# The last tile's final norm: channels-by-tokens with a broadcast factor, or tokens-by-channels with one factor per partition

## The chip, the cores and the metric

The kernel runs on one core of one Trainium2 chip. The metric is the device time of one execution in microseconds (us); lower is better. Before the change it is 2097.62 us, the median of three runs (2097.12 to 2098.48).

## The reference, cut to what matters

One inference step of a one-layer decoder: 2048 prompt tokens (behind 16 learned meta tokens) and 8 sample tokens, each a vector of 1024 channels in float32. A layer norms the input, projects it, runs sliding-window attention beside a depthwise convolution, adds the result back, and goes through a two-matrix feed-forward block (1024 to 4096 to 1024). What the change touches is the last line for both groups of tokens:

```
def rmsnorm(x, g):
    xf = x.astype(jnp.float32)
    y = xf * lax.rsqrt(jnp.mean(xf * xf, axis=-1, keepdims=True) + EPS)
    return (y * g.astype(jnp.float32)).astype(x.dtype)

    x = x + hid @ w_down                                # end of the layer
    y_prompt = rmsnorm(xp, norm_f_g)[:, N_META:]
    y_sample = rmsnorm(xs, norm_f_g)
```

Each token has one factor, the reciprocal root of the mean of its 1024 squares; each channel has one gain `g`.

## The kernel before, in words

Activations lie transposed: channels on the 128 partitions (8 chunks of 128 for 1024 channels), tokens along the row. The 2056 tokens that go out are cut into five tiles of 384, 448, 448, 448 and 328 tokens (the last one holds 320 prompt tokens and the 8 sample tokens). Weights come as 128x1024 slabs, 424 of them, through SP's queue; each is split into a high and a low float32r part (`whi` by ScalarE, `wlo` by VectorE), and `pe_step` runs 24 matmuls with one slab into one PSUM bank.

The tiles go through the feed-forward block one after the other. Work that isn't TensorE's main stream (attention, convolution, norms) is written as generators that are advanced between the matmuls; a scheduler then sets each engine's order by priority and readiness. For the last tile nothing is left to run beside it at the end: after the last `down_step` the program runs the final norm alone.

`down_step` (g = 3) adds the last partial result to the residual `y = s["x2"][d]` on VectorE (L115, `t<-mm,t`), once for each of the 8 chunks, and counts `s["ydone"]`. `final_gen` of the last tile follows: `norm_stats` squares each chunk on ScalarE (L134, `m<-t`) and sums the squares on VectorE (L115, `ss`). `rstd` in its quick form then takes three blocks of at most 128 tokens: matmuls of `ss` with a column of ones put the sum of each token on a partition of its own (`st<-ones,ss`), ScalarE takes the root (`rq<-st,epst`), VectorE the reciprocal (L130), ScalarE scales an identity with it (`m<-idn,rq`), matmuls with ones spread the factors over all partitions (`st<-m,ones`), and ScalarE copies them to `rs` (L138). At last VectorE multiplies each chunk by gain and factor (L119, `t<-t,sm,rs`, 8 times 128x328), and each chunk is stored as 128 rows of 328 tokens, from SP's and ScalarE's queue in turn (L934, `y_out<-t`). The host puts the chunks back in order after the run.

A PSUM pool of 8 banks is shared: `mm` (3 banks, the main stream), `pt` and `s` (2 each, attention), `st` (1, small results). `bias` (128x2048) and `p` are buffers of the attention.

Of the kernel before, what the change touches and what calls it, by code (L numbers as in the profile page):

```python
# [7 lines left out]
F32 = mybir.dt.float32  # L8
F32R = mybir.dt.float32r
AF = mybir.ActivationFunctionType  # L10
ALU = mybir.AluOpType
PSUM = bass.MemoryType.PSUM

D = 1024
SEQ = 2048
NMETA = 16
NSMP = 8
# [9 lines left out]
NT = len(PT)  # L27
RT = [PT[i] + (NSMP if i == NT - 1 else 0) for i in range(NT)]
# [3 lines left out]
YO = [8 * sum(RT[:i]) for i in range(NT)]  # L32
TM = max(TI)
# [8 lines left out]
G1, G2, GF, CWT, CB, LG, LB, SK, SKR = 0, 8, 16, 24, 148, 152, 156, 160, 168  # L42
# [3 lines left out]
STEP = "step"  # L46
# [30 lines left out]
            self.step(DRAIN)  # L77


def trunk(tc, x_in, w_all, smalls, rel, ck, cv, sconv, y_out, kv_out, ck_out, cv_out, up_out, us_out):  # L80
    nc = tc.nc
    with ExitStack() as ctx:
        cp = ctx.enter_context(tc.tile_pool(name="cp", bufs=1))
        tp = ctx.enter_context(tc.tile_pool(name="tp", bufs=NSLOT))
        tm = ctx.enter_context(tc.tile_pool(name="tm", bufs=NTMP))
        sl = ctx.enter_context(tc.tile_pool(name="sl", bufs=3))
        at = ctx.enter_context(tc.tile_pool(name="at", bufs=1))
        dr = ctx.enter_context(tc.tile_pool(name="dr", bufs=1, space=bass.MemoryType.DRAM))
        pm = ctx.enter_context(tc.tile_pool(name="pm", bufs=3, space=PSUM))
        pa = ctx.enter_context(tc.tile_pool(name="pa", bufs=2, space=PSUM))  # L90
        p1 = ctx.enter_context(tc.tile_pool(name="p1", bufs=1, space=PSUM))

        def ahead(gen, off, cond=None):
            while True:
                try:
                    if off and (cond is None or cond()):
                        with tc.high_priority(off):
                            r = next(gen)
                    else:
                        r = next(gen)  # L100
                except StopIteration:
                    return
                yield r
# [13 lines left out]
        def stt(out, a, s, b, op0, op1):  # L117
            dcost(out, 0.06)
            return nc.vector.scalar_tensor_tensor(out, a, s, b, op0=op0, op1=op1)  # L119
# [23 lines left out]
        def slot(dt=F32, i=None):  # L143
            t = tp.tile([128, TS], dt, tag="t", name="t")
            return t[:, SHIFT[i]:] if i in SHIFT else t
# [15 lines left out]
        sm = tm.tile([128, NSMALL], F32, tag="sm", name="sm", bufs=1)  # L161
# [3 lines left out]
        idn = cp.tile([128, 128], F32, name="idn")  # L165
        make_identity(nc, idn)
        ones = cp.tile([128, 128], F32, name="ones")
        nc.vector.memset(ones, 1.0)
        epst = cp.tile([128, 1], F32, name="epst")
# [3 lines left out]
        bias = cp.tile([128, NH, 256], F32, name="bias")  # L173
# [37 lines left out]
        bg = Background(clock)  # L211
# [105 lines left out]
        def run_stats(gen, box):  # L317
            for r in gen:
                if r is None or r is STEP:
                    yield r  # L320
                else:
                    box.append(r)

        def norm_split(chunks, n, gcol, hi, lo, ready=None, quick=False, i=None):
            box = []
            yield from run_stats(norm_stats(chunks, n, ready, quick), box)
            rs = box[0]
            prev = None
            def fin(p):
                c, h = p  # L330
                tt(lo[c][:, :n], h[:, :n], f(hi[c][:, :n]), ALU.subtract)

            for c in range(8):
                h = tmp()
                stt(h[:, :n], chunks[c][:, :n], sm[:, gcol + c:gcol + c + 1], rs[:, :n], ALU.mult, ALU.mult)
                hi.append(slot(F32R, i))
                lo.append(slot(F32R, i))
                cpy(hi[c][:, :n], h[:, :n])
                yield
                if prev is not None:  # L340
                    fin(prev)
                    yield
                prev = (c, h)
            fin(prev)

        st = [dict() for _ in range(NT)]
# [12 lines left out]
        def norm1_gen(i):  # L359
            x = st[i]["x"] = load_x(i)  # L360
            yield STEP
            st[i]["h1h"], st[i]["h1l"] = [], []
            yield from norm_split(x, TI[i], G1, st[i]["h1h"], st[i]["h1l"], quick="a%d" % i in QUICK, i=i)

        def norm1_first():
# [22 lines left out]
            s["rs"] = slot()  # L388
            for _ in ahead(run_stats(norm_stats(x, n, quick="a0" in QUICK, gate=s["h1h"][7], out=s["rs"]), box), 2000):
                pass  # L390
# [330 lines left out]
        def conv_gen(i):  # L721
# [66 lines left out]
            yield STEP  # L788
            if "m%d" % i in QUICK:
                ps = misc(i < LNM)  # L790
# [20 lines left out]
            box = []  # L811
            yield from run_stats(rstd(ssum, r, 1.0 / 512, "l%d" % i in QUICK, i < LNM), box)
            rs = box[0]
# [66 lines left out]
        def norm2_gen(i):  # L880
            s = st[i]
            s["h2h"], s["h2l"] = [], []
            while "x2" not in s:
                yield STEP
            yield from norm_split(s["x2"], RT[i], G2, s["h2h"], s["h2l"], ready=lambda c: len(s["x2"]) > c,
                                  quick="b%d" % i in QUICK, i=i)

# [20 lines left out]
        def down_step(i, g, d, budget):  # L908
# [10 lines left out]
                flush()  # L919
            pe_step([t[:, :n] for t in s["hh"]], [t[:, :n] for t in s["hl"]], n, ev, budget, late=d == 0)  # L920

        def final_gen(i):
            s = st[i]
            n = RT[i]
            s.setdefault("ydone", 0)
            box = []
            yield from run_stats(norm_stats(s["x2"], n, ready=lambda c: s["ydone"] > c,
                                             quick="f%d" % i in QUICK), box)
            rs = box[0]
            for c in range(8):  # L930
                y = s["x2"][c]
                stt(y[:, :n], y[:, :n], sm[:, GF + c:GF + c + 1], rs[:, :n], ALU.mult, ALU.mult)
                q = (nc.sync, nc.scalar)[c % 2] if i == NT - 1 else nc.gpsimd
                q.dma_start(y_out[:, YO[i] + c * n:YO[i] + (c + 1) * n], y[:, :n])  # L934
                yield

        def bias_setup():
# [78 lines left out]
        for op in prog:  # L1016
# [6 lines left out]
            elif op[0] == "ff":  # L1023
                _, i, t, g, k = op
# [3 lines left out]
        gens = {}  # L1028
        nin = 0
        cat_alloc(0)  # L1030
        for op in prog:
            k = op[0]
            if k == "in":
                _, i, m = op
                if i == 0:
                    if nin == N1AT:
                        gens["n1"] = [bg.add(g1)]
                    if nin == BAT:
                        bias_setup()
                    nin += 1  # L1040
                win_step(i, m, 24 * (TI[i] / 2400.0) - 1.2 - 0.6, spare=i == 0 and nin in (4, 5))
            elif k == "in2":
                m = op[1]
                win_step(0, m, 24 * (TI[0] / 2400.0) - 1.2 - 0.6, keep=True)
                win_step(1, m, 24 * (TI[1] / 2400.0) - 0.6)
            elif k == "conv0":
                flush()
                gens["conv"] = [bg.add(ahead(conv_gen(0), HP0, lambda: "ln" in st[0])), bg.add(conv_pe_gen(0), True)]
            elif k == "attn0":
                flush()  # L1050
                gens["attn"] = [bg.add(attn_gen(0, range(j, PT[0] // BQ[0], NS0)), A0F) for j in reversed(range(NS0))]
            elif k == "out":
                _, i, m = op
                wout_step(i, m, ff_budget(i, False))
            elif k == "ff":
                _, i, t, g, c = op
                b = ff_budget(i, t == "u")
                if t == "u":
                    up_step(i, g * 8 + c, b)
                else:  # L1060
                    down_step(i, g, c, b)
            elif k == "bg":
                i = op[1]
                flush()
                cat_alloc(i)
                gens["attn"] = [bg.add(attn_gen(i, range(j, PT[i] // BQ[i], NS1))) for j in range(NS1)]
                if i == NT - 1:
                    gens["attn"].append(bg.add(sample_gen(i)))
                gens["conv"] = [bg.add(ahead(conv_gen(i), HPC, lambda: "ln" in st[i]))]
            elif k == "sync_bg":  # L1070
                flush()
                bg.drain(gens["attn"] + gens["conv"])
            elif k == "n1":
                gens["n1"] = [bg.add(norm1_gen(op[1]))]
            elif k == "sync_n1":
                bg.drain(gens["n1"])
            elif k == "n2":
                gens["n2"] = [bg.add(ahead(norm2_gen(op[1]), HPN if op[1] else HPN0))]
            elif k == "sync_n2":
                flush()  # L1080
                bg.drain(gens["n2"])
            elif k == "fin":
                gens["fin"] = [bg.add(ahead(final_gen(op[1]), HPF if op[1] == NT - 1 else 0))]
                if op[1] == NT - 1:
                    flush()
                    bg.drain()
# [14 lines left out]
HPC = 0  # L1101
HPN = 0
HPN0 = 300
HPF = 0
COV = 5
BAT = 1
WARM = 12
N1AT = 3
A0F = True
QUICK = ["a0", "a1", "l0", "m0", "b0", "f4"]  # L1110
NS0 = 2
NS1 = 1
NPB = 2
# [6 lines left out]
def _pack(inp):  # L1120
# [62 lines left out]


_OUTS = [
    ("y_out", (128, 8 * sum(RT))), ("kv_out", (128, 2, 128 + NSMP)), ("ck_out", (128, 1024)),
    ("cv_out", (128, 1024)), ("up_out", (128, 4, CW - 1)), ("us_out", (128, 4, NSMP, CW)),
]

# [38 lines left out]
```

## Time and profile before

| | us |
|---|---|
| median of three runs | 2097.62 |
| the profiled execution, its own time | 2097.54 |
| its span, first to last instruction | 2095.7 |
| TensorE matmul busy | 2068.3 (99%) |
| weight loads busy | 1961.5 (94%) |
| VectorE busy | 1525.2 (73%) |
| ScalarE busy | 1181.0 (56%) |
| DMA queue of SP, share of 16 engines' span | 32.5% |

The span runs from the first to the last instruction; the execution's own time is 1.84 us longer. Busy times can overlap between engines. TensorE's granted clock is full in nearly all of the span (mean 0.993). The end of the span, where TensorE has no more of its main stream, is a few microseconds long and is too short to be seen in these shares.

### The profile page before, as it was taken

What the parts mean: (1) busy time and instruction counts of PE and PEld (TensorE: products, weight loads), DVE (VectorE), ACT (ScalarE), POOL (GpSimd) and SP (SyncE); (2) the same over time, 40 slices, a digit from 0 to 9 for tenths busy, and PEclk for the clock granted to TensorE, in tenths of its full rate; (3) what the DMA queues carried; (4) which work ended last, traced back from release to release, by engine and by line L of the source; (5) the groups of instructions that cost most, each with busy time, mean ns of one, the idle gap of its engine ahead of it and who ended that gap; (6) DMA issues with size and microseconds to landing.
All of it is one profiled execution on the core that took longest, in us unless ns stands there. A gap on an engine that the chain in (4) does not pass through costs nothing.

```text
span 2095.7 us, 30054 instructions
## 1 busy us (share of the span) xinstructions
PE 2068.3 (99%) x11354; PEld 1961.5 (94%) x11354; DVE 1525.2 (73%) x2603; ACT 1181.0 (56%) x2154; POOL 55.8 (3%) x111
## 2 busy tenths in 40 slices
PE   9899999999999999999999999999999999999998
PEld 8688899999999999999999999999999999999997
DVE  7896798977858987658669886567797754564444
ACT  7577565667456456564454647555646465454443
POOL 3000000000000000000000000000011000000000
PEclk9899999999999999999999999999999999999999
DMA  7113233334532222234323222244433322444443
GB/s 209 47 37 111 100 122 104 128 114 160 179 111 101 101 101 101 101 136 162 129 104 108 101 101 101 101 172 150 142 117 112 123 105 101 151 162 151 151 143 105
DMA packets 77536, 254.39 MB, mean 121 GB/s; under 512 B 9661, under 2 KB 20037, under 8 KB 77392
## 3 DMA queue, kind: packets, MB, share of 16 engines
q1 hardware_dynamic: 72000, 238.08, 32.5%
q0 software_dynamic: 4672, 13.65, 2.3%
q8 instruction: 89, 1.46, 0.3%
q10 hardware_dynamic: 720, 0.76, 0.1%
q14 instruction: 55, 0.45, 0.1%
HBM read 241.97 MB, written 10.47 MB: 120 GB/s over the span
## 4 chain that ended last, share of the span: by engine, by line
PE 95%; DVE 2%; DMA 1%; ACT 1%; issue 0%; POOL 0%; SPq 0%; DVEq 0%; ACTq 0%; POOLq 0%
PE mm L159 89%; PE st L159 2%; PE pt L595 1%; PE s L159 1%; DVE t L119 1%; DMA bias<-skw 0%; DMA skw<-t 0%; DVE t L115 0%; PE cps L159 0%; DVE m L119 0%; ACT p L135 0%; DMA raw<-w_all 0%; DVE p L576 0%; DMA sm<-smalls 0%; ACT L134 0%
## 5 line engine op out<-in xcount | busy, mean ns | idle before, releaser
L159 PE MATMUL mm<-t,whi 128*128 128x448 f32 (+3 forms) x6560 | 1330.9, 349 | 3.1 <-ACT t L138 0.8
L159 PEld LDWEIGHTS mm<-t,whi 128*128 128x128 f32 x6560 | 1164.1, 188 | 58.2 <-DVE t L115 2.9
L138 ACT CAST whi<-raw 128x1024 fp32r<-128x1024 f32 x424 | 443.5, 1049 | 546.6 <-PE mm L159 430.2
L159 PE MATMUL mm<-t,wlo 128*128 128x448 f32 (+3 forms) x3280 | 702.6, 347 | 0.0
L115 DVE TENSOR_TENSOR wlo<-raw,whi 128x1024 fp32r<-128x1024 f32 x424 | 516.6, 1218 | 224.7 <-PE mm L159 123.5
L159 PEld LDWEIGHTS mm<-t,wlo 128*128 128x128 f32 x3280 | 587.9, 188 | 24.9
L119 DVE SCALAR_TENSOR_TENSOR t<-u,sm,t 128x448 f32<-128x448 f32 (+1 forms) x480 | 300.5, 645 | 3.5
L115 DVE TENSOR_TENSOR t<-mm,t 128x448 f32<-128x448 f32 (+2 forms) x200 | 116.5, 583 | 184.5 <-PE mm L159 181.4
L115 DVE TENSOR_TENSOR t<-m,t 128x448 fp32r<-128x448 f32 (+3 forms) x236 | 134.1, 581 | 25.8 <-ACT t L138 25.1
L138 ACT CAST t<-m 128x448 fp32r<-128x448 f32 (+3 forms) x236 | 125.3, 536 | 18.8 <-DVE m L119 14.6
L134 ACT ACTIVATE m<-mm 128x448 f32<-128x448 f32 (+2 forms) x176 | 90.2, 512 | 51.0 <-PE mm L159 49.5
L134 ACT ACTIVATE m<-t 128x448 f32<-128x448 f32 (+3 forms) x140 | 71.7, 542 | 61.7 <-DVE t L115 43.0
L134 ACT ACTIVATE m<-m 128x448 f32<-128x448 f32 (+3 forms) x164 | 90.1, 549 | 4.5 <-DVE m L115 0.6
L135 ACT ACTIVATE p<-p,nm 112x240 f32<-112x240 f32 (+3 forms) x152 | 72.3, 477 | 27.3 <-DVE nm L124 25.9
L576 DVE CUSTOM_DVE_ANT_0 p<-s,bias,sm 112x240 f32<-112x240 f32 (+3 forms) x152 | 61.1, 449 | 6.2 <-DMA bias<-skw 3.8
L134 ACT ACTIVATE p<-p,rd 112x240 f32<-112x240 f32 (+3 forms) x152 | 61.9, 476 | 3.9 <-DVE rd L130 3.5
L115 DVE TENSOR_TENSOR ss<-ss,m 128x448 f32<-128x448 f32 (+3 forms) x100 | 58.4, 584 | 6.3 <-ACT m L134 2.8
L934 POOL DMA_DIRECT2D y_out<-t x32 | 17.3, 543 | 1602.6 <-DVE t L119 1601.4
L130 DVE RECIPROCAL rs<-m 128x448 f32<-128x448 f32 (+2 forms) x15 | 41.6, 2776 | 23.9 <-ACT m L134 23.9
L119 DVE SCALAR_TENSOR_TENSOR t<-t,sm 128x384 f32<-128x384 f32 (+1 forms) x98 | 58.3, 612 | 0.9
L159 PE MATMUL mm<-cal,whi 128*128 128x448 f32 (+2 forms) x160 | 55.3, 347 | 0.2 <-DVE cal L115 0.2
L159 PE MATMUL mm<-cah,whi 128*128 128x448 f32 (+2 forms) x160 | 55.3, 347 | 0.0
(178 smaller groups left out, 1159.6 us busy)
## 6 DMA issues: line engine op xcount, KB each, us to landing
raw<-w_all SPq DMA_DIRECT2D x424, 512.0 KB, 3.2
t<-x_in SPq DMA_DIRECT2D x40, 224.0 KB, 4.6
y_out<-t POOLq DMA_DIRECT2D x24, 224.0 KB, 3.3
t<-x_in SPq DMA_DIRECT2D x16, 164.0 KB, 3.5
t<-x_in POOLq DMA_DIRECT2D x8, 224.0 KB, 4.3
t<-x_in SPq DMA_DIRECT2D x8, 200.0 KB, 4.6
t<-x_in SPq DMA_DIRECT2D x8, 192.0 KB, 3.8
y_out<-t POOLq DMA_DIRECT2D x8, 192.0 KB, 4.7
```

What stands on the lines that cost most here:

```text
L115: return nc.vector.tensor_tensor(out, a, b, op=op)
L119: return nc.vector.scalar_tensor_tensor(out, a, s, b, op0=op0, op1=op1)
L130: return nc.vector.reciprocal(out, a)
L134: return nc.scalar.activation(out, a, f, bias=bias, scale=scale)
L135: return nc.scalar.activation(out, a, f, bias=bias, scale=scale, accum_out=accum_out)
L138: return nc.scalar.copy(out, a)
L159: return nc.tensor.matmul(out, lhsT, rhs, start=start, stop=stop)
L576: nc.vector.tensor_tensor_reduce(out=p[:bq, c, :nk], in0=sp[c // 2][:bq, c % 2, :nk], in1=bias[:bq, h, b0:b0 + nk], scale=1.0, scalar=sm[: ...
L595: nc.tensor.transpose(t[:r, c * bq:(c + 1) * bq], p[:bq, c, a:a + r], idn[:bq, :bq])
L934: q.dma_start(y_out[:, YO[i] + c * n:YO[i] + (c + 1) * n], y[:, :n])
```

## The change

For the last tile alone, `final_last` takes the place of `final_gen`. The 328 tokens are read as three blocks of 110 tokens, which begin at 0, 109 and 218 and so overlap by one token each. Each chunk, once squared, is multiplied by its gain (ScalarE for chunks 0 to 6, in place; VectorE for chunk 7, into a new buffer), and TensorE turns it, block by block, into six PSUM banks that hold tokens on partitions and 512 channels along the row. The sums per token are formed as before by matmuls with a column of ones, but from the running sum of seven chunks and the eighth chunk's squares apart; root and reciprocal are taken once for three columns. The factors are not spread: they scale the six banks directly, one factor per partition, three banks on ScalarE and three on VectorE, into old attention buffers. Six stores follow, each of 109, 109 or 110 rows (tokens) of 512 channels, into a new output `yl_out` that has tokens as rows. Chunks 0 to 3 are turned as they come, 4 to 7 behind the sums (three one-element copies order them). Other tiles are as before.

```
+            w = -(-n // 3)
+            at0 = [0, w - 1, n - w]
+            rows = [w - 1, n - 2 * w + 1, w]
+            tb = [[pa.tile([128, 512], F32, tag="pt", name="yt"), pa.tile([128, 512], F32, tag="s", name="yt")],
...
+            def turn(c):
+                for b in range(3):
+                    nc.tensor.transpose(tb[b][c // 4][:w, c % 4 * 128:c % 4 * 128 + 128], yg[c][:, at0[b]:at0[b] + w],
+                                        idn)
+            for c in range(8):
...
+                with tc.high_priority(400 if c == 7 else 0):
+                    act(sq[:, :n], y[:, :n], AF.Square)
...
+                if c == 7:
+                    yg.append(tmp())
+                    ts(yg[c][:, :n], y[:, :n], g, None, ALU.mult)
+                else:
+                    act(y[:, :n], y[:, :n], AF.Copy, scale=g)
...
+                elif 1 < c < 7:
+                    tt(ssum[:, :n], ssum[:, :n], sq[:, :n], ALU.add)
+                if c < 4:
+                    turn(c)
+                yield
+            r = at.tile([128, 4], F32, tag="rq", name="rq", bufs=2)
+            with tc.high_priority(400):
+                ps = misc()
+                for b in range(3):
+                    o = slice(at0[b], at0[b] + w)
+                    mm(ps[:w, b:b + 1], ssum[:, o], ones[:, 0:1], True, False)
+                    mm(ps[:w, b:b + 1], sqs[7][:, o], ones[:, 0:1], False, True)
+                act(r[:w, :3], ps[:w, :3], AF.Sqrt, bias=epst[:w], scale=1.0 / D)
+                recip(r[:w, :3], r[:w, :3])
+            for b in range(3):
+                nc.vector.tensor_copy(tb[b][1][:1, :1], sqs[7][:1, :1])
+            for c in range(4, 8):
+                turn(c)
...
+            k = 0
+            for h in range(2):
+                for b in range(3):
+                    o = bl[:w, k * 512:k * 512 + 512] if k < 4 else pl[:w, (k - 4) * 512:(k - 4) * 512 + 512]
+                    if k % 2 == 0:
+                        act(o, tb[b][h][:w], AF.Copy, scale=r[:w, b:b + 1])
+                    else:
+                        ts(o, tb[b][h][:w], r[:w, b:b + 1], None, ALU.mult)
+                    q = nc.scalar if k == 4 else nc.sync
+                    q.dma_start(yl_out[at0[b]:at0[b] + rows[b], h * 512:h * 512 + 512], o[:rows[b]])
+                    k += 1
...
-                q = (nc.sync, nc.scalar)[c % 2] if i == NT - 1 else nc.gpsimd
-                q.dma_start(y_out[:, YO[i] + c * n:YO[i] + (c + 1) * n], y[:, :n])
+                nc.gpsimd.dma_start(y_out[:, YO[i] + c * n:YO[i] + (c + 1) * n], y[:, :n])
```

## Rows read from the trace of the kernel before

**Rows 1.** The page: busy time and share of each engine.
```profile
span 2095.7 us, 30054 instructions
PE 2068.3 (99%) x11354; PEld 1961.5 (94%) x11354; DVE 1525.2 (73%) x2603; ACT 1181.0 (56%) x2154; POOL 55.8 (3%) x111
```

**Rows 2.** Busy time by stretch of the end: engines, PEclk, DMA share, GB/s.
```profile
2060.00:2083.76 23.76, 23.75 (x159) 23.48 (x157) 12.08 (x18) 8.18 (x12) 0.00 (x0) 1.00 0.20 67
2083.76:2085.44 1.68, 0.00 (x0) 0.00 (x1) 1.00 (x2) 0.48 (x1) 0.00 (x0) 1.00 0.00 0
2085.44:2088.65 3.21, 1.72 (x12) 1.49 (x12) 0.30 (x3) 1.78 (x6) 0.00 (x0) 1.00 0.00 0
2088.65:2092.50 3.85, 0.00 (x0) 0.00 (x0) 3.85 (x8) 0.00 (x0) 0.00 (x0) 0.52 0.63 220
2092.50:2094.03 1.53, 0.00 (x0) 0.00 (x0) 0.00 (x1) 0.00 (x0) 0.00 (x0) 0.50 0.93 325
2094.03:2095.70 1.67, 0.00 (x0) 0.00 (x0) 0.00 (x0) 0.00 (x0) 0.00 (x0) 0.50 0.00 0
```

**Rows 3.** Timeline of the end: start, us, engine, line, instruction, idle before.
```profile
2082.39 1.36 PE L159 MATMUL mm<-t,wlo 128*128 128x328 f32 x8
2083.78 0.50 DVE L115 TENSOR_TENSOR t<-mm,t 128x328 f32<-128x328 f32 x1 [2.05 <-PE mm L159]
2084.38 0.48 ACT L134 ACTIVATE m<-t 128x328 f32<-128x328 f32 x1 [3.18 <-DVE t L115]
2084.89 0.50 DVE L115 TENSOR_TENSOR ss<-ss,m 128x328 f32<-128x328 f32 x1 [0.60 <-ACT m L134]
...
2085.44 0.74 PE L159 MATMUL st<-ones,ss 128*128 128x1 f32 x6 [1.69 <-DVE ss L115]
2086.22 0.41 ACT L134 ACTIVATE rq<-st,epst 128x2 f32<-128x2 f32 x2 [1.36 <-PE st L159]
2086.51 0.30 DVE L130 RECIPROCAL rq<-rq 128x2 f32<-128x2 f32 x2 [1.12 <-ACT rq L134]
...
2087.16 0.98 PE L159 MATMUL st<-m,ones 128*128 128x128 f32 x6 [0.99 <-ACT m L134]
2088.18 0.43 ACT L138 COPY rs<-st 128x328 f32<-128x328 f32 x1 [0.53 <-PE st L159]
2088.65 3.85 DVE L119 SCALAR_TENSOR_TENSOR t<-t,sm,rs 128x328 f32<-128x328 f32 x8 [1.84 <-ACT rs L138]
2089.23 3.16 SPq L934 DMA_DIRECT2D y_out<-t  x4
2089.71 3.16 ACTq L934 DMA_DIRECT2D y_out<-t  x4
```

**Rows 4.** Timeline of TensorE where two float32 blocks are turned.
```profile
1704.26 0.36 PE L159 MATMUL mm<-t,whi 128*128 128x448 f32 x1
1704.46 0.27 PE L543 MATMUL st<-idn,vt 128*128 128x128 f32 x1
1704.57 0.27 PE L544 MATMUL st<-idn,vt 128*80 128x128 f32 x1
```

**Rows 5.** Groups by shape, 512 columns read from PSUM: count, busy, mean ns.
```profile
L138 ACT CAST ph<-pt 128x512 fp32r<-128x512 f32 x10 | 5.6, 581 | 2.8 <-PE pt L595 2.8
L115 DVE TENSOR_TENSOR pl<-pt,ph 128x512 fp32r<-128x512 f32 x10 | 6.8, 684 | 2.1 <-ACT ph L138 2.1
```

**Rows 6.** DMA from 2084 to 2100 us: rate in 40 slices, queues, issues.
```profile
DMA  0000000000000007999999997000000000000000
q1 hardware_dynamic: 576, 0.67, 12.0%
q10 hardware_dynamic: 576, 0.67, 12.0%
...
y_out<-t SPq DMA_DIRECT2D x4, 164.0 KB, 1.9
y_out<-t ACTq DMA_DIRECT2D x4, 164.0 KB, 1.9
```

**Rows 7.** The page, DMA queue of SP: packets, MB, share of 16 engines over the span.
```profile
q1 hardware_dynamic: 72000, 238.08, 32.5%
```

**Rows 8.** DMA from 4.6 to 5.1 us, while `relt` (33 rows) is loaded.
```profile
DMA packets 142, 0.20 MB, mean 405 GB/s; under 512 B 37, under 2 KB 131, under 8 KB 142
q1 hardware_dynamic: 110, 0.15, 80.5%
q0 software_dynamic: 32, 0.05, 27.2%
```

**Rows 9.** DMA issues over the whole span: KB, median us to landing.
```profile
relt<-rel POOLq DMA_DIRECT2D x1, 50.5 KB, 4.3
```

More of the change, by code (lines that the diff above doesn't have):

```diff
@@ L77, in drain, with trunk @@
             self.step(DRAIN)
-def trunk(tc, x_in, w_all, smalls, rel, ck, cv, sconv, y_out, kv_out, ck_out, cv_out, up_out, us_out):
+def trunk(tc, x_in, w_all, smalls, rel, ck, cv, sconv, y_out, yl_out, kv_out, ck_out, cv_out, up_out, us_out):
     nc = tc.nc
@@ L920, in down_step, with final_last @@
             pe_step([t[:, :n] for t in s["hh"]], [t[:, :n] for t in s["hl"]], n, ev, budget, late=d == 0)
+        def final_last(i):
+            s = st[i]
+            n = RT[i]
+            s.setdefault("ydone", 0)
+            w = -(-n // 3)
+            at0 = [0, w - 1, n - w]
+            rows = [w - 1, n - 2 * w + 1, w]
+            tb = [[pa.tile([128, 512], F32, tag="pt", name="yt"), pa.tile([128, 512], F32, tag="s", name="yt")],
+                  [pa.tile([128, 512], F32, tag="pt", name="yt"), pm.tile([128, 512], F32, tag="mm", name="yt")],
+                  [pa.tile([128, 512], F32, tag="s", name="yt"), pm.tile([128, 512], F32, tag="mm", name="yt")]]
+            ssum = tm.tile([128, TM], F32, tag="ss", name="ss", bufs=2)
+            sqs = []
+            yg = []
+            def turn(c):
[3 more added lines that the diff above has]
+            for c in range(8):
+                while s["ydone"] <= c:
+                    yield STEP
+                y = s["x2"][c]
+                g = sm[:, GF + c:GF + c + 1]
+                sq = tmp()
+                with tc.high_priority(400 if c == 7 else 0):
+                    act(sq[:, :n], y[:, :n], AF.Square)
+                sqs.append(sq)
+                if c == 7:
[3 more added lines that the diff above has]
+                    act(y[:, :n], y[:, :n], AF.Copy, scale=g)
+                    yg.append(y)
+                if c == 1:
+                    tt(ssum[:, :n], sqs[0][:, :n], sq[:, :n], ALU.add)
+                elif 1 < c < 7:
[16 more added lines that the diff above has]
+                turn(c)
+            bl = bias.rearrange("p h x -> p (h x)")
+            pl = at.tile([128, 4, 256], F32, tag="p", name="p", bufs=NPB).rearrange("p h x -> p (h x)")
+            k = 0
[9 more added lines that the diff above has]
+                    k += 1
@@ L1082, in trunk @@
             elif k == "fin":
-                gens["fin"] = [bg.add(ahead(final_gen(op[1]), HPF if op[1] == NT - 1 else 0))]
+                gens["fin"] = [bg.add((final_last if op[1] == NT - 1 else final_gen)(op[1]))]
                 if op[1] == NT - 1:
@@ L1103 @@
 HPN0 = 300
-HPF = 0
 COV = 5
@@ L1109 @@
 A0F = True
-QUICK = ["a0", "a1", "l0", "m0", "b0", "f4"]
+QUICK = ["a0", "a1", "l0", "m0", "b0"]
 NS0 = 2
@@ L1185 @@
 _OUTS = [
-    ("y_out", (128, 8 * sum(RT))), ("kv_out", (128, 2, 128 + NSMP)), ("ck_out", (128, 1024)),
+    ("y_out", (128, 8 * sum(RT[:-1]))), ("yl_out", (RT[-1], D)), ("kv_out", (128, 2, 128 + NSMP)), ("ck_out", (128, 1024)),
     ("cv_out", (128, 1024)), ("up_out", (128, 4, CW - 1)), ("us_out", (128, 4, NSMP, CW)),
@@ L1210 @@
     y = r["y_out"]
-    yt = [y[:, YO[i]:YO[i] + 8 * RT[i]].reshape(128, 8, RT[i]).transpose(2, 1, 0).reshape(RT[i], D) for i in range(NT)]
-    yt = np.concatenate(yt, 0)
+    yt = [y[:, YO[i]:YO[i] + 8 * RT[i]].reshape(128, 8, RT[i]).transpose(2, 1, 0).reshape(RT[i], D) for i in range(NT - 1)]
+    yt = np.concatenate(yt + [r["yl_out"]], 0)
     y_prompt = np.ascontiguousarray(yt[None, :SEQ])
```

## The prediction, made before the changed kernel ran

> **What bounds the kernel now.** I read the page first: TensorE is busy for 2068.3 of 2095.7 us [rows 1], so an edit counts only where it lengthens or shortens TensorE's stream or the stretch behind it. Then the busy times by stretch [rows 2]: up to 2083.76 TensorE works 23.75 of 23.76 us; behind that stand 11.94 us in which it has 1.72 us of work. The change lies in these 11.94 us. The timeline [rows 3] gives their order as one chain: last add to the residual (2083.78), square (2084.38), add to `ss`, sums per token (2085.44), root, reciprocal, identity scaled, factors spread (2087.16), copied (2088.18), eight multiplications (2088.65 to 2092.50) with a store behind each. The stores are nearly saturated: from 2090.0 on the 16 DMA engines are 90% busy and more [rows 6], at 325 GB/s in the last stretch, and their last data pass at 2094.03. From there to the end of the span are 1.67 us of waiting for the last store and shutting down [rows 2]. Outside the span lie 1.84 us (2097.54 less 2095.70).
>
> **The change on the way to the first store.** Base is the profiled execution.
> - The last matmul ends at 2083.76, the add to the residual at 2084.28, chunk 7's square at 2084.86 [rows 3]: unchanged. The last add to `ss` (0.50 us) goes, because chunk 7's squares enter the sums by themselves.
> - The seven multiplications by the gain on ScalarE (0.48 us each, by the square of the same shape) cost nothing: it is busy for 8.18 of the 23.76 us before the end [rows 2]. Without that cover they would cost 0.48 us for the last. VectorE's one for chunk 7 (0.50) runs beside the square.
> - Turning: a block turned in float32 starts 0.11 us after the one before (1704.46 to 1704.57) and is through 0.27 us after its start [rows 4]. The twelve of chunks 0 to 3 take 12 x 0.11 = 1.3 us. TensorE is full until 2083.76 and empty from there to 2085.44, so they run in that gap, to about 2085.1. If they were put between the matmuls, the main stream would be 1.3 us longer. From above a float32 matmul of 128 columns bounds them: 0.98 us for three [rows 3], 0.33 each, twelve in 4.0 us. I take 0.11, because those rows are turns themselves.
> - Sums: three tokens-per-partition sums took 0.74 us in six records [rows 3]; now there are twelve records, 1.5 us by that row, 1.2 if the first pair is done early. From 2085.1 to about 2086.4. The square is ready at 2084.86, so the gap's turns hold them up by 0.2 us.
> - Root and reciprocal, once for three columns: 0.27 and 0.18 us with the handing-on, by the first of each pair in [rows 3]: 2086.9. Turns of chunks 4 to 7 run beside this, 2086.4 to 2087.9; the three one-element copies (some 0.15 each, by the small reciprocals' 0.30 for two) are on VectorE in the gap before.
> - Gone: identity, spreading and copy (2086.69 to 2088.65, 1.96 us) and the eight multiplications (3.85). In their place six scalings of 512 columns out of PSUM, three by engine: 0.58 on ScalarE, at most 0.68 on VectorE (the row reads two operands) [rows 5]. The first ends at 2087.5, the last near 2089.3.
> - An issue stands 0.1 us behind its scaling, and data passed about 0.9 us after the issue began (2089.23 to 2090.1, [rows 3, 6]). The first store's data pass at 2088.5; before it was 2090.1. So far the change is 1.6 us ahead.
>
> **The stores.** This is the term that decides. The bytes are the same, 1.34 MB, in six stores in place of eight. What is new is the count of rows: 109, 109 and 110 where all stores of before have 128. How many engines share a store of 109 rows the trace doesn't show, and it has to be bounded. Each store of before makes 144 packets (576 for four) [rows 6]: 128 rows and 16 small ones, so 16 engines with eight rows each. The one load with an odd count is `relt`, 33 rows, 50.5 KB [rows 9]: while it runs, exactly 11 packets of 2 KB or more pass (142 less 131) [rows 8], that is 11 shares of three rows. Both fit equal shares on the largest number of engines up to 16 that divides the rows: 16 x 8, 11 x 3. Shares rounded up fit too (33/16 rounded up is 3), but no transfer of the trace shows a share smaller than its neighbours, and `relt` came through the software queue. 109 is a prime: equal shares are had on one engine alone. 110 gives 11 engines with 10 rows.
>
> [...]
>
> The price of one engine: SP's queue took 32.5% of 16 x 2095.7 us for 238.08 MB, 45.8 us of one engine per MB [rows 7], and the last stores the same (12.0% of 16 x 16 us for 0.67 MB, [rows 6]); `relt` took 27.2% of 16 x 0.5 us for 0.0517 MB, 42.1 us per MB [rows 8]; a sixteenth of the highest mean rate, 405 GB/s in the same stretch, is 39.5. Four stores of 109 rows x 2048 bytes are 0.893 MB, and the two stores of 110 rows bring another 20 rows, 0.041 MB, to the same engine. 0.934 MB take 36.9 to 42.8 us; I take 42.1 us per MB, 39.3 us, the row in the middle. The bound below is an even spread: 3.9 us, as before (2090.1 to 2094.03).
>
> Forecast: 2088.5 + 39.3 + 1.67 + 1.84 = 2131.3 us, and 0.08 more for the median over the profiled run: 2131. Fifteen engines idle while one moves rows; no other engine of the core has anything left to do, so nothing hides it. With the price's ends and 2 us for the path and for a lone engine's pace, its own range is 2125 to 2137.
>
> **Rivals.**
> - Even spread (not slower). Rows that don't divide are shared out rounded up, 7 to an engine. For it: `relt` fits that too, and 16 engines carry everything else. Against it: no unequal share in the trace. The first data pass 1.6 us earlier and 1.34 MB take 3.9 us: 2088.5 + 3.9 + 1.67 + 1.84 = 2095.9, within 0.2%. The last scaling, near 2089.3, doesn't set the end then: its store would be through by 2089.4 + 0.9 + 0.7 = 2091.0, before the 2092.4 of the whole. The point from which it decides: the change breaks even when the fullest engine is done 5.5 us after 2088.5 (2094.03), some 0.13 MB or 64 rows; four odd stores stay under that if each runs on seven engines or more.
> - One engine for each odd store, but another one each time. 0.223 MB take 9.4 us; the last odd store (ScalarE's third scaling, done near 2088.7) has data from 2089.7, ends at 2099.1, total 2102.6: slower by 0.24%. For it: nothing in the rows says which engine takes a lone share.
> - The turning is dear. With an even spread, 24 turns at 0.33 us put the sums off by 2.7 us and the last bank by as much again: 2095.9 + 5.4 = 2101.3. Against it: the turns of [rows 4].
> - Clearly faster. It takes 4.2 us off; the path gives 1.6, and the stores ahead are 3.9 us of nearly busy engines, so the transfers would have to take a third of their time.
>
> **How the numbers follow.** Equal shares on one common engine 0.70, even spread 0.20, another engine each 0.05, dear turns 0.03, clearly faster 0.02. 0.2% (4.2 us) is about what a measurement of this kernel tells from no change: slower 0.75, within 0.23, faster 0.02. As 2125 to 2137 holds at most 0.7, the range goes down to the even spread: 2095 to 2137.
>
> **What would show it.** In the profile after, the DMA share behind the last scaling would stand near 1/16 for some 38 us, at 22 to 25 GB/s, with all other engines idle, and the stores of 109 rows would make 110 packets where 128 rows made 144. The first store's issue at 2087.6, turns of 0.11 us in the gap, twelve sum records and no `st<-m,ones` would show the path right. A DMA share near 0.9 at over 300 GB/s behind the last scaling would make the prediction wrong.

## The result, and the profile after

The changed kernel takes 2128.84 us (median of four runs, 2128.18 to 2129.54) where the kernel before takes 2097.73 on the same chip: the ratio is 1.0148, with a 95% interval of 1.0131 to 1.0166. It is 31 us slower. The profiled execution took 2128.47 us, 1.77 us more than its span.

The page: TensorE's busy time is within 0.4 us of [rows 1], with 24 more matmuls, the turns; what grew is the span.
```profile
span 2126.7 us, 30100 instructions
PE 2068.7 (97%) x11378; PEld 1963.6 (92%) x11378; DVE 1523.2 (72%) x2600; ACT 1184.7 (56%) x2159; POOL 55.6 (3%) x111
```

Busy time by stretch, in the columns of [rows 2] (length; busy time and count of PE, PEld, DVE, ACT, POOL; PEclk, DMA share, GB/s).
```profile
2060.00:2082.92 22.92, 22.92 (x155) 22.91 (x155) 11.62 (x18) 11.75 (x19) 0.00 (x0) 1.00 0.20 69
2082.92:2085.82 2.90, 2.90 (x32) 2.90 (x30) 1.34 (x6) 0.74 (x3) 0.00 (x0) 1.00 0.00 0
2085.82:2087.95 2.13, 0.81 (x8) 0.56 (x6) 2.06 (x3) 1.84 (x3) 0.00 (x0) 1.00 0.02 4
2087.95:2107.00 19.05, 0.00 (x0) 0.00 (x0) 0.00 (x1) 0.00 (x0) 0.00 (x0) 0.54 0.07 24
2107.00:2117.00 10.00, 0.00 (x0) 0.00 (x0) 0.00 (x0) 0.00 (x0) 0.00 (x0) 0.50 0.15 49
2117.00:2125.30 8.30, 0.00 (x0) 0.00 (x0) 0.00 (x0) 0.00 (x0) 0.00 (x0) 0.50 0.14 47
2125.30:2126.70 1.40, 0.00 (x0) 0.00 (x0) 0.00 (x0) 0.00 (x0) 0.00 (x0) 0.50 0.00 0
```
By 2087.95 all computing is over, 5.0 us behind the last matmul (2082.93); before it took 8.7 us. Then no engine works, and for 19 us the DMA share is 0.07, one engine in sixteen, at 24 GB/s, where [rows 2] has 0.93 and 325 GB/s.

Timeline of the end, the counterpart of [rows 3] (start, us, engine, line, instruction, idle before).
```profile
2081.57 1.36 PE L159 MATMUL mm<-t,wlo 128*128 128x328 f32 x8
2082.63 0.94 PEld L938 LDWEIGHTS yt<-idn,t 128*110 128x110 f32 x8
2082.77 1.04 PE L938 MATMUL yt<-idn,t 128*110 128x128 f32 x8
2082.97 0.50 DVE L115 TENSOR_TENSOR t<-mm,t 128x328 f32<-128x328 f32 x1 [2.06 <-PE mm L159]
2083.51 0.48 ACT L134 ACTIVATE m<-t 128x328 f32<-128x328 f32 x1 [2.52 <-DVE t L115]
...
2084.94 0.33 PE L159 MATMUL st<-ones,m 128*110 128x1 f32 x2
...
2085.31 0.26 ACT L134 ACTIVATE rq<-st,epst 110x3 f32<-110x3 f32 x1 [1.32 <-PE st L159]
...
2085.60 0.18 DVE L130 RECIPROCAL rq<-rq 110x3 f32<-110x3 f32 x1 [1.32 <-ACT rq L134]
...
2085.82 1.26 ACT L134 ACTIVATE bias<-yt,rq 110x512 f32<-110x512 f32 x2 [0.24 <-DVE rq L130]
2085.89 1.41 DVE L124 TENSOR_SCALAR bias<-yt,rq 110x512 f32<-110x512 f32 x2
...
2086.53 21.05 SPq L987 DMA_DIRECT2D yl_out<-bias  x4
```
The early turns fill the gap at 0.11 us each, the sums end 2.3 us behind the last matmul, root and reciprocal follow, and the first store is issued at 2086.53, 3.6 us behind the last matmul; before it was 5.5. The path is what the change says. The last line is the odd one: from SP's first issue to the end of its fourth pass 21 us, where [rows 3] has 3.16 for four.

DMA from 2084 to 2130 us, the counterpart of [rows 6] (rates in 40 slices; then by queue packets, MB, share of 16 engines).
```profile
GB/s 0 0 4 11 14 18 25 27 25 25 27 25 27 25 25 27 25 25 27 25 118 112 25 27 25 25 27 25 85 144 25 25 27 25 27 23 0 0 7 0
DMA packets 683, 1.35 MB, mean 29 GB/s; under 512 B 26, under 2 KB 26, under 8 KB 682
q1 hardware_dynamic: 572, 1.12, 7.3%
q10 hardware_dynamic: 110, 0.22, 1.2%
```
The packet counts name the shares, read as one small packet by engine (stores of 128 rows made 16 of them at a DMA share of 0.93 [rows 2, 6]). ScalarE's queue (q10) carries one store of 109 rows: 110 packets, 109 rows and one small one, so one engine. SP's 572 are three such stores (330) and two of 110 rows at 121 each (242): 110 rows and 11 small ones, so 11 engines. That the lone engine is one and the same for both queues is seen between 2090 and 2107 us:
```profile
DMA packets 212, 0.43 MB, mean 25 GB/s; under 512 B 1, under 2 KB 1, under 8 KB 212
q1 hardware_dynamic: 118, 0.24, 3.6%
q10 hardware_dynamic: 94, 0.19, 2.9%
```
Stores of both queues are under way, yet 212 packets take 17 us, one every 80 ns, and from 2092 on rows of the two queues take turns. Together they fill 6.5% of 16 engines, 1.04 of one. The stores of 110 rows have a share on it too, by their small packets: ten of the first one's eleven pass from 2108.38 to 2108.87, the last at 2115.84, 0.81 us, ten rows, behind that of the second store of 109 (2115.03); the second one's pass from 2117.81 to 2118.31 and at 2125.37, 0.80 us behind that of the third store of 109 from SP (2124.57).

### The profile page after: what moved, and what is told of

It reads as the page before. It is cut to its first block, busy times and chain, and to the rows that moved or that the text cites. A ratio compares the mean times of both kernels' runs of the same rounds, so it can differ in the third digit from the quotient of the medians.

```text
span 2126.7 us, 30100 instructions
## 1 busy us (share of the span) xinstructions
PE 2068.7 (97%) x11378; PEld 1963.6 (92%) x11378; DVE 1523.2 (72%) x2600; ACT 1184.7 (56%) x2159; POOL 55.6 (3%) x111
## 4 chain that ended last, share of the span: by engine, by line
PE 94%; DVE 2%; DMA 1%; ACT 1%; issue 0%; POOL 0%; SPq 0%; DVEq 0%; ACTq 0%; POOLq 0%
PE mm L159 88%; PE st L159 2%; PE s L159 1%; PE pt L595 1%; DVE t L119 1%; DMA bias<-skw 0%; PE cps L159 0%; DMA skw<-t 0%; ACT p L135 0%; DVE m L119 0%; DMA raw<-w_all 0%; DVE p L576 0%; DVE t L115 0%; DMA sm<-smalls 0%; ACT L134 0%
```

## The experiments

The theory, the author's reading of these packets (109 rows and 1 small one, 110 and 11, 128 and 16): a store from a hardware queue is cut into equal shares, on the largest number of engines up to 16 that divides its rows, always from the same engine on. The rival: these stores are slow whatever their count, because of what else is new in them (rows of tokens, 2 KB pieces 4 KB apart, other buffers).

**e1: another cut.** Blocks 112 wide, stored as 104, 112 and 112 rows.
```
-            w = -(-n // 3)
-            at0 = [0, w - 1, n - w]
-            rows = [w - 1, n - 2 * w + 1, w]
+            w = 112
+            at0 = [0, n - 2 * w, n - w]
+            rows = [n - 2 * w, w, w]
```


> The changed kernel with one edit: the three blocks are 112 tokens wide and are stored as 104, 112 and 112 rows. Equal shares (104 = 13 x 8, 112 = 16 x 7): the fullest engine moves 2 x 8 + 4 x 7 = 44 rows of about 83 ns, 3.7 us in place of 38; with the path of the changed kernel (first data 4.3 us after the last matmul, 1.4 us from the last data to the end of the span, 1.8 us outside) 2094 to 2096 us, faster than before by 2 to 3 us. Rival, stores of token rows out of these buffers are slow whatever their count (rows of 2 KB with a step of 4 KB in DRAM, another source buffer): no change, 2126 to 2130 us.

Measured: 2095.93 us (11 runs) beside 2097.04, ratio 0.9994, interval 0.9985 to 1.0003. The 31 us are gone with the cut alone (blocks two tokens wider, other counts of rows), and the rival falls. The stretch in which the stores' data pass, and the queues:
```profile
2086.84:2092.47 5.63, 0.00 (x0) 0.00 (x0) 0.65 (x1) 0.35 (x1) 0.00 (x0) 0.80 0.81 239
```
```profile
q1 hardware_dynamic: 618, 1.11, 23.4%
q10 hardware_dynamic: 128, 0.23, 5.0%
```
128 packets are 112 rows and 16 small ones; 618 are three of these and two of 117 (104 and 13). So far as expected. But 0.81 x 16 x 5.63 are 73 us of engine time for 656 rows, 111 ns a row instead of the 83 I had put, and the data pass for 5.6 us, not 3.7.

**e2: even counts that 16 doesn't divide.** Blocks of 110, stored as 110, 108 and 110 rows.
```
-            at0 = [0, w - 1, n - w]
-            rows = [w - 1, n - 2 * w + 1, w]
+            at0 = [0, w, n - w]
+            rows = [w, n - 2 * w, w]
```


> The changed kernel with one edit: blocks of 110 tokens are stored as 110, 108 and 110 rows, none a multiple of 16. Equal shares (110 = 11 x 10, 108 = 12 x 9): the fullest engine moves 4 x 10 + 2 x 9 = 58 rows, 4.8 us, 16 engines never all at work: 2095 to 2097.5 us, about 1.2 us behind the cut of 104, 112, 112, and the data pass at most at 11 to 12 sixteenths of the full rate. Rounded shares (7 rows an engine): as the cut of 104, 112, 112, at the full rate. Rival of slow token rows: 2126 to 2130 us.

Measured: 2097.53 us, ratio 1.0001, interval 0.9992 to 1.0010: no difference from the kernel before, and 1.6 us behind e1.
```profile
2086.73:2093.93 7.20, 0.00 (x0) 0.00 (x0) 0.63 (x1) 0.34 (x1) 0.00 (x0) 0.75 0.60 187
```
```profile
q1 hardware_dynamic: 604, 1.12, 22.5%
q10 hardware_dynamic: 120, 0.22, 4.6%
```
120 packets are 108 rows and 12 small ones; 604 are four of 121 and one of 120. The DMA share of 0.60 is some 10 of 16 engines. Rounded shares are excluded for these stores from hardware queues: eleven and twelve small packets each, not sixteen.

**e3: the same odd counts from POOL's software queue.**
```
-                    q = nc.scalar if k == 4 else nc.sync
+                    q = nc.gpsimd
```


> The changed kernel with one edit: all six stores, still 109, 109 and 110 rows, are issued from POOL's software queue. If the software queue rounds shares up (7 rows an engine): the fullest engine moves 42 rows, 3.5 us; with 0.54 us for an issue in place of 0.33 and a later start 2095 to 2099 us. If it makes equal shares like the hardware queue: 38 us on one engine, 2126 to 2131 us.

Measured: 2097.62 us, ratio 1.0002, interval 0.9993 to 1.0011. Stores of 109 rows, and no 38 us:
```profile
DMA packets 481, 1.35 MB, mean 85 GB/s; under 512 B 106, under 2 KB 106, under 8 KB 480
q0 software_dynamic: 480, 1.34, 26.8%
```
```profile
2088.10:2093.60 5.50, 0.00 (x0) 0.00 (x0) 0.00 (x0) 0.00 (x0) 2.17 (x4) 0.67 0.76 240
```
480 less 106 are 374 packets of data, for 656 rows. If one holds up to two rows, shares of seven rows rounded up give just that: 109 rows are 15 engines of 7 (4 packets each) and one of 4 (2 packets), 62 packets, four times; 110 rows are 15 engines of 7 and one of 5, 63, twice. So `relt` [rows 8, 9], which came through the software queue, was no evidence for equal shares: 33 rows rounded up give the same 11 x 3.

**e4: the odd count without the change.** The kernel before, its last eight stores of 128 rows cut into 127 and 1.
```
-                q.dma_start(y_out[:, YO[i] + c * n:YO[i] + (c + 1) * n], y[:, :n])
+                o = slice(YO[i] + c * n, YO[i] + (c + 1) * n)
+                if i == NT - 1:
+                    q.dma_start(y_out[:127, o], y[:127, :n])
+                    q.dma_start(y_out[127:, o], y[127:, :n])
+                else:
+                    q.dma_start(y_out[:, o], y[:, :n])
```


> The kernel before with one edit: each of its eight last stores is cut into one of 127 rows and one of one row (1312 bytes each); nothing is turned. Equal shares: 127 is a prime, so 8 x 127 rows of 56 to 60 ns pass on one engine, 57 to 61 us from 2090.1 on: 2150 to 2154 us. Rounded shares (8 rows an engine): 2097 to 2099 us. Rival of slow token rows: 2097 to 2099 us too, because these rows are channels.

Measured: 2153.71 us, one run, 56.7 us behind the kernel before. Nothing is turned here, and the rows are channels of 1312 bytes:
```profile
2099.00:2139.00 40.00, 0.00 (x0) 0.00 (x0) 0.00 (x0) 0.00 (x0) 0.00 (x0) 0.50 0.07 22
```
One engine at 22 GB/s for the whole stretch, and the eight stores of 127 rows and eight of one make 16 small packets in all, one each (1040 packets, 1024 rows). Neither the turning nor the new output is needed for the loss: the count of rows makes it.

**Where e1's gain stays.** e1 issues its first store 1.9 us nearer to the last matmul than the kernel before, but its data pass for 5.6 us where they passed for 3.9. Three runs ask why a row takes 111 ns. e5 takes blocks of 128 (`w = 128`, stores of 72, 128 and 128 rows); e6 keeps e1's cut and lays the output out as two halves of 512 channels, so that the rows of a store have no gaps in DRAM; e8 has both, and the first seven chunks' sums ahead in columns of their own.

e6's edit:
```
-                    q.dma_start(yl_out[at0[b]:at0[b] + rows[b], h * 512:h * 512 + 512], o[:rows[b]])
+                    q.dma_start(yl_out[h * n + at0[b]:h * n + at0[b] + rows[b]], o[:rows[b]])
```
e8's sums:
```
+                for t, e in ((ssum, 0), (sqs[7], 4)):
+                    for b in range(3):
+                        mm(ps[:w, e + b:e + b + 1], t[:, at0[b]:at0[b] + w], ones[:, 0:1], True, True)
+                cpy(r[:w, :3], ps[:w, 0:3])
+                tt(r[:w, :3], ps[:w, 4:7], r[:w, :3], ALU.add)
```


> The changed kernel with blocks of 128 tokens, stored as 72, 128 and 128 rows (12 engines with 6 rows, 16 with 8). Compared with the cut of 104, 112, 112, where the data passed for 5.6 us, from 4.4 to 10.1 us behind the last matmul, at 110 ns a row in place of 83. If the slower rows come from shares of 7 rows that lie across the partitions otherwise than the 8 of a 128-row store: rows of 83 to 92 ns again, 4 to 4.3 us of passing, some 2094.5 us in all. If they come from how the rows lie in DRAM (2 KB pieces, 4 KB apart) or from all stores being queued at once: 5.4 to 5.8 us as before, some 2096 us.

> The changed kernel with the cut of 104, 112, 112 rows, and an output laid out as two halves of 512 channels, so that the rows of a store follow one another in DRAM without a gap (the host joins the halves). If the gaps in DRAM make the rows slow: 83 to 92 ns a row, 4 to 4.3 us of passing, some 2094.5 us. If the shares of 7 rows or the crowd of queued stores do: 5.4 to 5.8 us of passing, some 2096 us.

> Both edits together (72, 128, 128 rows; output in two halves), and the sums of the first seven chunks formed ahead in columns of their own and added to those of the eighth. If either cause holds, rows of 83 to 92 ns; if neither (the crowd of queued stores), 5.4 us of passing still. The sums should bring the first data 0.3 us nearer to the last matmul (4.1 in place of 4.4 us). 2093.8 to 2095.8 us, faster than the kernel before by 1.3 to 3.3 us.

Measured: e5 2095.38 us (ratio 0.9991, 0.9982 to 1.0000), e6 2095.90 (0.9995, 0.9985 to 1.0004), e8 2095.86 (0.9994, 0.9985 to 1.0003), beside 2097.24. The stretches of e5:
```profile
2087.00:2088.50 1.50, 0.00 (x0) 0.00 (x0) 0.76 (x2) 0.46 (x1) 0.00 (x0) 1.00 0.81 268
2088.50:2090.00 1.50, 0.00 (x0) 0.00 (x0) 0.00 (x0) 0.00 (x0) 0.00 (x0) 0.63 1.02 358
2090.00:2092.10 2.10, 0.00 (x0) 0.00 (x0) 0.00 (x0) 0.00 (x0) 0.00 (x0) 0.50 0.61 193
```
and of e6:
```profile
2087.10:2092.55 5.45, 0.00 (x0) 0.00 (x0) 0.59 (x1) 0.29 (x1) 0.00 (x0) 0.66 0.84 246
```
e6 spends 0.84 x 16 x 5.45 = 73 us of engine time, as e1: the gaps in DRAM cost nothing. e5 spends 64.4 us (0.81, 1.02 and 0.61 of its stretches), 98 ns a row, and its middle stretch runs at 358 GB/s, above the 325 of [rows 2]. So the cut has a part in it, but e5 falls between its two forecasts: 98 ns and 5.0 us of passing, where 83 to 92 ns and 4 to 4.3 us were expected if shares of seven rows were the cause.

The mean hides what happens. By the trace's packets the median row takes 84 ns in e1, e5 and e6, as on the lone engine. What raises the mean are rows of over 100 ns: 164 of 656 in e1, the longest 869 ns, and 98 in e5; the kernel before has none over 78 ns among its 1024 shorter ones. Counted in the order of SP's queue, e5's first store of 72 rows has a mean of 119 ns, the two stores of 128 behind it 86 and 88 ns, and most of these pass with all 16 engines at work. So neither every row of a small share nor the crowd of engines is slow as such. (A row of 1312 bytes, too, took 61 ns with all engines at work in the kernel before, 3.91 us for the 64 rows of an engine, and 60 on e4's lone engine, 61.0 us for 1024.) What the slow rows wait for stays open.

e8's rows took 97 ns and its data passed for 4.9 us, as in e5, so the two edits together give no more than the cut, and its time lies just above the range expected. Its sums are a miss. They end earlier, but a copy and an addition come between them and the root:
```profile
2085.06 0.16 ACT L138 COPY rq<-st 128x3 f32<-128x3 f32 x1 [1.49 <-PE st L159]
...
2085.25 0.16 DVE L115 TENSOR_TENSOR rq<-st,rq 128x3 f32<-128x3 f32 x1 [1.38 <-ACT rq L138]
...
2085.45 0.30 ACT L134 ACTIVATE rq<-rq,epst 128x3 f32<-128x3 f32 x1 [0.23 <-DVE rq L115]
```
In that trace the first data pass 5.0 us behind the last matmul, in e5's 4.6; the edit lost 0.4 us where I expected 0.3 gained.

**e9: the store of 72 rows as 64 and 8; e10: e5 once more.**
```
+                    for lo, hi in ((0, rows[b] // 64 * 64), (rows[b] // 64 * 64, rows[b])):
+                        if hi > lo:
+                            q.dma_start(yl_out[at0[b] + lo:at0[b] + hi, h * 512:h * 512 + 512], o[lo:hi])
```


> The cut of 72, 128, 128 rows with each store of 72 rows made as two, of 64 and of 8 rows (16 engines with 4 rows; 8 engines with one). There the data passed for 5.0 us at 97 ns a row, with 350 to 400 GB/s at first and 200 to 250 near the end. If the slow part is the 12 engines' shares of 6 rows: below 90 ns a row, 4.2 to 4.6 us of passing, some 0.5 us nearer: 2094.3 to 2095.3 us. If the end is slow because its last stores come late, or because two queues mix: 5 us still, 2095 to 2095.8 us.

> The cut of 72, 128, 128 rows once more, beside the kernel before on this chip: faster than before by 1.4 to 2.4 us (ratio 0.9989 to 0.9993), data passing for 4.8 to 5.1 us at some 97 ns a row.

Measured: e9 2095.68 us (ratio 0.9992, 0.9983 to 1.0001), e10 2095.24 (0.9989, 0.9981 to 0.9998), beside 2097.16. e9's transfers are denser,
```profile
2088.05:2092.45 4.40, 0.00 (x0) 0.00 (x0) 0.38 (x1) 0.09 (x1) 0.00 (x0) 0.63 0.92 305
```
than e10's,
```profile
2088.20:2093.10 4.90, 0.00 (x0) 0.00 (x0) 0.45 (x1) 0.15 (x1) 0.00 (x0) 0.80 0.79 267
```
by 0.5 us. But the rows are no cheaper: 0.92 x 16 x 4.40 are 64.8 us, 99 ns a row, where below 90 was expected if the twelve engines' shares of six rows were the slow part. That theory falls. By equal shares e9 has 42 rows on the fullest engine in place of 44; whether that is the 0.5 us isn't shown. Its data also start later behind the last matmul (4.9 us, 4.6 in e10), and the times of the two can't be told apart. e10 is 1.9 us under the kernel before, as expected, with an interval (0.4 to 4.0 us) that just leaves out zero; e5, the same kernel, has one that ends at zero. Both are some 33 us under the changed kernel.

## Why the prediction was right

- **The stores on one engine: right.** The term was 39.3 us, from 2088.5 on; the data pass from 2087.31 to 2125.38, 38.1 us, without a gap between packets. The price taken, 42.1 us per MB, was a little high: 0.934 MB in 38.1 us are 40.8, between the bounds of 39.5 and 45.8 that [rows 7, 8] gave; from 2090 on, at 80 ns for 2048 bytes, it was 39.1, and slow rows of up to 540 ns at the start made most of the rest. The rows of before had not decided between equal and rounded shares: 16 x 8 and 11 x 3 fit both, as the prediction says itself, so these rows don't carry 0.70 against 0.20. Nor does any row of before show the one common engine, or the 20 rows that the stores of 110 bring to it; both were the author's estimate. The changed kernel showed them: 110 packets for 109 rows and 121 for 110, rows of both queues in turn on one engine, and the eleventh shares of ten rows there in 0.81 and 0.80 us. e1 and e2 agree on the shares, with 128 packets for 112 rows and 120 for 108 (which of the engines it is, no run shows). From the software queue, e3's 374 data packets fit rounded shares.
- **The path to the first store: right in its steps, 1.2 us too long.** Behind the last matmul the first issue came after 3.6 us (3.84 by the prediction) and the first data after 4.4 (4.7). The other 0.8 us are the last matmul itself, which ended at 2082.93 and not at 2083.76. That lead doesn't come from the change: the first store of a finished tile stood as far ahead already, in the kernel before
```profile
L934 POOL DMA_DIRECT2D y_out<-t x32: 539/542/583, 561.1 to 1879.1; - x32
```
and in the changed one (the last column is the first and the last start).
```profile
L1001 POOL DMA_DIRECT2D y_out<-t x32: 539/539/582, 560.3 to 1878.3; - x32
```
- **The scalings were dearer.** 512 columns took 0.68 us on ScalarE and 0.74 on VectorE (0.58 and 0.68 by [rows 5]). The first one's 0.1 us lie in the path above; the stores hide the others.
- **The end: 1.32 us** behind the last data, not 1.67, and 1.77 outside the span, not 1.84. Sum: 2087.31 + 38.07 + 1.32 + 1.77 = 2128.47. All four terms of the forecast were a little too long, 2.8 us together.
- **Two slips that the sum doesn't rest on.** With the price's ends and 2 us the range of the one engine begins at 2127, not at 2125. Three scalings of 0.68 us behind 2086.9 end at 2088.9, not near 2089.3; they ended at 2087.95.
- **The rivals.** The even spread fell for these stores from the hardware queues (DMA share 0.07) and fits those from the software queue (e3, 0.76). Another engine for each odd store fell by the rate of 25 GB/s with both queues' stores under way. The turns were as cheap as [rows 4]. The rival's time of 2095.9 for a spread that keeps all engines busy was about what e1 and e5 then took, 2095.93 and 2095.38, though by another sum: the path a little shorter, the transfers longer by 1 to 1.7 us.
- **Not in the prediction:** that an issue waits (below). It cost nothing here, because the full engine sets the end anyway: its packets follow one another without a gap from 2087.31 to 2125.38.

## What to carry to other kernels

In these runs a store from SP's or ScalarE's queue made as many shares as the largest divisor of its row count that isn't above 16, by the small packets: 128 and 112 rows 16 (144 and 128 packets), 104 rows 13 (117), 108 rows 12 (120), 110 rows 11 (121), 72 rows 12 (84), and the primes 109 (rows of 2048 bytes, 110 packets) and 127 (1312 bytes, 128 packets) one, at 25 and 22 GB/s. Loads with odd counts were not tried; before a store from these queues, look for that divisor, and count its packets in the trace. From POOL's queue the odd stores took 2097.62 us, with the 374 data packets of rounded shares (e3). A cut that is natural for the arithmetic (328 tokens in three even parts) should be moved by a few rows, or overlapped, until that divisor is 16 or near it for each store. When a change brings the first store forward, look at the transfers too: in e1 it came 1.9 us nearer to the last matmul, and the data passed for 5.6 us where they had passed for 3.9.

## What the runs showed of the hardware that was not expected

An instruction that only issues a DMA held its queue for up to 18.1 us. In the changed kernel the issues from SP (durations as min/median/max):
```profile
L987 SPq DMA_DIRECT2D yl_out<-bias x4: 315/1220/18145, 2086.5 to 2107.0; - x4
L987 SPq DMA_DIRECT2D yl_out<-p x1: 8740/8740/8740, 2107.6 to 2107.6; - x1
```
SP's third store, of 110 rows, took 18.1 us to issue (from 2088.8), while the lone engine worked on the two stores of 109 ahead of it; its fifth, of 110 too, took 8.7 us. Ten of their eleven engines were idle meanwhile (DMA share 0.07 from 2088.8 to 2106.9 and from 2109.5 to 2116.3), and their data came only around 2107 and 2117, the two humps in the rate above. In e4 it was the one-row stores behind those of 127 rows whose issue took up to 14.4 us. SP issued nothing else in these times: its fourth store, whose scaling had ended at 2087.30, was issued at 2106.96.

For the same bytes, stores of 104 and 112 rows (e1) took 13% more engine time than stores of 72 and 128 (e5), by more rows that take over 100 ns. Their place in DRAM isn't the cause (e6, without gaps, took the same 73 us), and shares of four rows in place of six don't cure it (e9: its first 72 rows have a mean of 145 ns). e5's second and third store, of 128 rows, had few of them (means of 86 and 88 ns); what such rows wait for stays open.
